# A decoder layer on one core: 96 instead of 64 tokens of the second group gather their experts, and 72 instead of 56 expert chunks run ahead of the second product

## The chip, the cores and the metric

The kernel runs on one core of one Trainium2 chip. TensorE (PE) multiplies matrices, VectorE (DVE), ScalarE (ACT) and GpSimd (POOL) do elementwise work, SyncE (SP) mostly issues DMAs, and sixteen DMA engines move data between HBM and the core's memories. The metric is device microseconds of one execution, from three runs. Each kernel's profile comes from one further execution.

## The reference, cut to what matters

One layer over 512 tokens of 2048 channels in f32: a mixer (pooling and attention heads in parallel), a cross attention over 256 memory tokens, and an expert layer (PEER), each added to x, and a last RMSNorm. The change lies mostly in PEER. For each token and each of 8 heads, two score vectors over 128 keys give the 16 best keys each, the 16 best sums of pairs give 16 experts of 16,384 (expert = key 1 x 128 + key 2) and a softmax over the 16 gives gates. With 128 experts k per token:

```python
a = jnp.einsum('td,tkd->tk', hb, jnp.take(w_u, ib, axis=0))
c = gb * jax.nn.gelu(a)
y = jnp.einsum('tk,tkd->td', c, jnp.take(w_v, ib, axis=0))
```

w_u and w_v are 16,384 x 2048 each, 134 MB. The attention rotates 32 of 128 channels of q and k by sines and cosines of the positions (rope).

## The kernel before, in words

**Two groups of tokens.** The first 128 tokens go through all layers first (row layout, from L370). The other 384 (`TR`) follow in a transposed layout `xT` (channels in partitions, 16 tiles `KD`).

**Two ways to do PEER.** *Gathering*: for a block of 128 rows, one indirect DMA fetches one expert row of 8 KB for each (1 MB in all, `rows`, L113), and DVE makes a dot product with the token (`dot0`, L318; `dot1`, L1075) or adds the scaled row to a sum in PSUM (`axpy0`, L331; `axpy1`, L1086). The first group does this for its 128 tokens: 128 dots, a turn with the GELU, 128 sums, an output step. Of the second group the first `NS` = 64 tokens do it too: each token stands in two rows (`SG` = 2), so 64 dots and 64 sums suffice. *Dense*: the other `ND` = 320 tokens are multiplied with all 16,384 experts, in 128 chunks of 128 experts, and a table of gates, zero for experts not chosen, masks the result.

**Products in three parts.** Each f32 weight tile of 128 x 1024 (`wraw`, 512 KB, four buffers, loaded by SP) is split into a high half (`wh`, ACT, L143) and a low half (`wl`, DVE or POOL, L144). `mm3` (L149 to L152) multiplies high by high, high by low, low by high. A w_u chunk (`proj_one`) has 48 such matmuls with `ND` moving columns, a group of w_v (8 chunks, 16 output tiles) has 384.

**Order of the stages of the second group.** Attention and pooling (`z_chunk`; the first group's pick, `pick0`, runs beside its start in steps of DVE), w_out, cross attention, the PEER query projection with its scores, and then:
- *Picks* (L1038 to L1061): for each of three blocks of 128 tokens, `pick` makes experts and gates on DVE, three transposes on PE bring them to row layout, and then `a_until` issues the next `KB` = 7 w_u chunks, whose GELU goes to DRAM (`gad`). Their low halves are made on POOL.
- *Gates* (L1105 to L1134): 80 steps of four tokens; DVE compares (L1114) and scales (L1116), PE multiplies (L1119), ACT stores (L1120), and the blocks go to DRAM (`gd`). The w_u chunks from 21 to `K1` = 56 run beside them.
- *Second product* (L1177 on): 16 groups of w_v, the groups of chunks 56 to 127 first. Beside a group the eight chunks of the next are prepared (`c_chunk`): for chunks from `K1` on, the w_u chunk itself; below, the activation is read back from `gad`. The gates come from `gd`. In the last group but one the gathered sums are transposed and added to `xT` (L1203 to L1210).

**The queue of gather steps.** `queue` (L342) is a list of closures, 258 for the first group and 131 for the second, and `behind(rate)` takes so many from it at places between the matmuls. `RATE` sets it by stage: 3.0 and 2.2 a chunk in attention and pooling (from the tenth chunk on), 2.5 in w_out, 2.0 in cross attention, 0.25 in the query projection and the picks, 1.2 in the gates and at the first eight chunks of the second product. After that, the rest is spread over the slots of the groups (16 a group), by 1.3 (`R2`) more than the mean in the groups that still carry w_u chunks (L1167 to L1170). Rows land in four buffers in turn: `x0`, `rowx` and a pool of two. From L1064 on POOL runs in program order; the other engines are ordered by the framework's planner.

**Sines.** `cosT` and `sinT` for rope are made at the start of the second group's attention (L757 to L767), right before the first use.

## Time and profile before

| | |
|---|---|
| median of 3 runs (lowest, highest) | 3175.05 us (3169.79, 3180.04) |
| profiled execution | 3175.37 us, span 3173.6 us |
| mean granted clock of PE | 0.968 |
| busy: PE, DVE, POOL, ACT | 93%, 76%, 45%, 41% |
| moved by DMA | 912.79 MB, mean 288 GB/s |
| queue 1, weights and stores (SP) | 471.21 MB |
| queue 0, gathers (POOL) | 402.68 MB |
| queue 10 (ACT) | 35.88 MB |

The profile shows one execution. "Busy" of PE counts pipelined matmuls, so two kernels' shares can't be compared with the peak; how far apart matmuls start is read from counts in a stretch. The granted clock is the share of 2.4 GHz that PE was given: 1 or, at 1.2 GHz, 0.5, and a mean between them over a stretch. The DMA share is the time that packets took, over the time of sixteen engines; packets that overlap can bring it a little over 1. In a row of windows, each engine has its busy time and, after an x, its count of instructions; PEclk, the DMA share and GB/s end the row. The line numbers are those of the kernel before.

### The profile page before, as it was taken

The numbers are of one execution on the slowest core, as the hardware profiler recorded it, in microseconds if no ns is written. First come the engines' busy times: TensorE is split into PE (matmuls) and PEld (weight loads), VectorE is DVE, ScalarE is ACT, GpSimd is POOL, SyncE is SP. The second block draws the span as 40 slices with busy tenths as digits, with TensorE's granted clock in tenths as the row PEclk, the third lists the DMA queues.
The fourth block names the chain that finished last, engine by engine and source line by source line (L and its number), as shares of the span: only waits on it lengthen the run. The fifth ranks groups of instructions, "written<-read, shape, count | busy, mean of one in ns | idle before, by whom it ended". The sixth has DMA issues, their size and how long they took to land.

```text
span 3173.6 us, 47405 instructions
## 1 busy us (share of the span) xinstructions
PE 2947.7 (93%) x18311; PEld 2832.5 (89%) x18311; DVE 2422.7 (76%) x3360; ACT 1298.6 (41%) x1789; POOL 1433.8 (45%) x826
## 2 busy tenths in 40 slices
PE   7999879998988997899998999999999999999997
PEld 5868769988978997899998999999999999899997
DVE  7797877798878579599894767777777678787756
ACT  5676534432344443355543333333433333233334
POOL 0000046644534665544546555555555554454532
PEclk9999989999989998999999999999999999999998
DMA  7886737888975344588888989999899999999953
GB/s 261 295 300 214 244 119 282 330 309 339 342 266 192 111 127 124 182 302 318 315 304 315 357 325 359 357 367 355 330 372 353 353 354 358 346 357 362 343 163 106
DMA packets 243521, 912.79 MB, mean 288 GB/s; under 512 B 23488, under 2 KB 85600, under 8 KB 192224
## 3 DMA queue, kind: packets, MB, share of 16 engines
q1 hardware_dynamic: 136304, 471.21, 42.2%
q0 software_dynamic: 55296, 402.68, 32.1%
q10 hardware_dynamic: 51696, 35.88, 3.7%
q8 instruction: 144, 2.36, 0.3%
q14 instruction: 81, 0.66, 0.1%
HBM read 874.22 MB, written 35.45 MB: 287 GB/s over the span
## 4 chain that ended last, share of the span: by engine, by line
PE 66%; DVE 20%; DMA 5%; issue 5%; ACT 2%; POOL 0%; ACTq 0%; POOLq 0%; DVEq 0%; SPq 0%
PE pm L150 11%; PE pm L152 11%; PE pm L151 11%; PE pa L152 9%; PE pa L150 9%; PE pa L151 9%; DVE wl L144 2%; DVE u L1114 2%; DVE oh L295 1%; DVE oh L293 1%; PE pm L400 1%; PE pm L401 1%; PE pm L399 1%; PE pa L1119 1%; DMA rows<-in_w_v_rows_dram,sidx 1%
## 5 line engine op out<-in xcount | busy, mean ns | idle before, releaser
L144 POOL TENSOR_TENSOR wl<-wraw,wh 128x1024 fp32r<-128x1024 f32 x369 | 930.5, 2526 | 1433.3 <-ACT wh L143 1401.4
L143 ACT ACTIVATE wh<-wraw 128x1024 fp32r<-128x1024 f32 (+1 forms) x658 | 693.7, 1058 | 1042.1 <-PE pm L151 467.0
L152 PE MATMUL pa<-ch,wl 128*128 128x320 f32 x2048 | 634.5, 312 | 25.4 <-DVE wl L144 23.5
L150 PE MATMUL pm<-dH,wh 128*128 128x320 f32 x2048 | 640.4, 313 | 15.0 <-DVE cl L1164 6.5
L152 PE MATMUL pm<-dH,wl 128*128 128x320 f32 x2048 | 640.6, 313 | 6.1 <-DVE wl L144 3.9
L150 PE MATMUL pa<-ch,wh 128*128 128x320 f32 x2048 | 636.7, 311 | 7.3 <-DVE xT L1193 4.7
L151 PE MATMUL pm<-dL,wh 128*128 128x320 f32 x2048 | 639.0, 312 | 0.0
L151 PE MATMUL pa<-cl,wh 128*128 128x320 f32 x2048 | 635.3, 310 | 0.0
L144 DVE TENSOR_TENSOR wl<-wraw,wh 128x1024 fp32r<-128x1024 f32 (+1 forms) x289 | 377.4, 1308 | 166.5 <-ACT wh L143 158.7
L152 PEld LDWEIGHTS pa<-ch,wl 128*128 128x128 f32 x2048 | 387.1, 189 | 30.4 <-DVE wl L144 28.1
L150 PEld LDWEIGHTS pm<-dH,wh 128*128 128x128 f32 x2048 | 389.2, 190 | 16.3 <-DVE cl L1164 6.8
L150 PEld LDWEIGHTS pa<-ch,wh 128*128 128x128 f32 x2048 | 388.3, 190 | 10.2 <-ACT ch L1163 5.2
L152 PEld LDWEIGHTS pm<-dH,wl 128*128 128x128 f32 x2048 | 389.3, 190 | 8.2 <-DVE wl L144 5.4
L151 PEld LDWEIGHTS pm<-dL,wh 128*128 128x128 f32 x2048 | 389.3, 190 | 0.0
L151 PEld LDWEIGHTS pa<-cl,wh 128*128 128x128 f32 x2048 | 388.1, 190 | 0.0
L150 PE MATMUL pm<-hH,wh 128*128 128x384 f32 x1024 | 355.9, 348 | 10.4 <-DVE k L811 3.4
L152 PE MATMUL pm<-hH,wl 128*128 128x384 f32 x1024 | 354.2, 347 | 10.5 <-DVE wl L144 10.5
L151 PE MATMUL pm<-hL,wh 128*128 128x384 f32 x1024 | 354.4, 346 | 5.2 <-DVE hL L874 4.4
L1193 DVE TENSOR_TENSOR xT<-pa,xT 128x320 f32<-128x320 f32 x256 | 124.7, 487 | 196.6 <-PE pa L152 191.0
L150 PEld LDWEIGHTS pm<-hH,wh 128*128 128x128 f32 x1024 | 197.6, 193 | 17.1 <-issue 5.8
L152 PEld LDWEIGHTS pm<-hH,wl 128*128 128x128 f32 x1024 | 197.6, 193 | 13.4 <-DVE wl L144 12.5
L151 PEld LDWEIGHTS pm<-hL,wh 128*128 128x128 f32 x1024 | 197.7, 193 | 6.9 <-DVE hL L874 4.7
(413 smaller groups left out, 4571.6 us busy)
## 6 DMA issues: line engine op xcount, KB each, us to landing
wraw<-in_w_u_dram SPq DMA_DIRECT2D x256, 512.0 KB
wraw<-in_w_v_dram SPq DMA_DIRECT2D x256, 512.0 KB
wraw<-in_w_in_dram SPq DMA_DIRECT2D x64, 512.0 KB
xT<-in_w_in_f_dram SPq DMA_DIRECT2D x63, 512.0 KB
gd<-stage SPq DMA_DIRECT2D x10, 2048.0 KB
gt<-gd ACTq DMA_DIRECT2D x32, 640.0 KB
wraw<-in_w_pq_f_dram SPq DMA_DIRECT2D x32, 512.0 KB
wraw<-in_w_out_dram SPq DMA_DIRECT2D x32, 512.0 KB
```

Of the source, the lines that this page charges most:

```text
L143: S.activation(wh[:, c], raw[:, c], AF.Copy)
L144: i = (lo_eng or V).tensor_tensor(wl[:, c], raw[:, c], wh.bitcast(F32)[:, c], op=ALU.subtract)
L150: TE.matmul(ps, wh, xh, start=start, stop=False)
L151: TE.matmul(ps, wh, xl, start=False, stop=False)
L152: TE.matmul(ps, wl, xh, start=False, stop=stop)
L293: V.tensor_tensor(oh, iota50.unsqueeze(1).broadcast_to([P, 16, NCAND]), cf[:, h, :].unsqueeze(2).broadcast_to([P, 16, NCAND]), op=ALU.is_e ...
L295: V.tensor_tensor(oh, oh, ecand[:, h, :].unsqueeze(1).broadcast_to([P, 16, NCAND]), op=ALU.mult)
L399: TE.matmul(ps, xh, wh, start=start, stop=False)
L400: TE.matmul(ps, xh, wl, start=False, stop=False)
L401: TE.matmul(ps, xl, wh, start=False, stop=stop)
L1114: V.tensor_tensor(u, iota.unsqueeze(1).unsqueeze(1).broadcast_to([P, 2, 4, P]), e12T[:, :, t:t + 4].unsqueeze(3).broadcast_to([P, 2, 4, P] ...
L1193: V.tensor_tensor(xT[:, dd, NS:], ps[:, :ND], xT[:, dd, NS:], op=ALU.add)
```

## The change

- `NS` goes from 64 to 96, `ND` from 320 to 288, and the gate blocks `NTB` from 10 to 9. The 96 tokens gather in two sets: 64 tokens in two rows each (64 dots, 64 sums) and 32 in four rows each (32 and 32). Each set starts by reading its repeated tokens from DRAM (`hyd`) and ends in a row buffer; the first set's sums are added after two dots of the second (`add1`).
- `K1` goes from 56 to 72 and `KB` from 7 to 9. In the picks, `a_until` now stands ahead of the transposes, which are ordered after the last matmul issued. A new rate, 0.5, holds for the chunks in the picks.
- The repeated tokens are made by POOL and ACT, not by DVE, and go to DRAM.
- `cosT` and `sinT` are made in the first group's PEER query projection.
- In `pick0` the product with the one-hot comparison runs on POOL.

```diff
-NS = 64
-SG = P // NS
-NK = P // SG
+SETS = ((0, 64), (64, 32))
+NS = sum(n for _, n in SETS)
-RATE = (3.0, 2.2, 2.5, 2.0, 0.25, 1.2)
+RATE = (3.0, 2.2, 2.5, 2.0, 0.25, 0.5, 1.2)
-K1, U0, GE = 56, 0, 2
-KB = 7
+K1, U0, GE = 72, 0, 2
+KB = 9
@@ mm3
-        TE.matmul(ps, wl, xh, start=False, stop=stop)
+        last_mm[0] = TE.matmul(ps, wl, xh, start=False, stop=stop)
@@ pick_steps (eng is G from pick0, V else)
-            V.tensor_tensor(oh, oh, ecand[:, h, :].unsqueeze(1).broadcast_to([P, 16, NCAND]), op=ALU.mult)
+            eng.tensor_tensor(oh, oh, ecand[:, h, :].unsqueeze(1).broadcast_to([P, 16, NCAND]), op=ALU.mult)
@@ the first group's PEER query projection (the lines at the attention's start go)
+        def pos_in():
+            posr.append(ep.tile([P, TR], F32, name="jk", bufs=2)[:32].bitcast(I32))
+            nc.scalar.dma_start(posr[0], a["positions"][:, T0:].broadcast_to([32, TR]))
+            nc.scalar.dma_start(invf, a["invfreq"])
+        def trig_rows():
+            V.tensor_copy(cosT, posr[0])
+            V.tensor_scalar(cosT, cosT, scalar1=invf, scalar2=None, op0=ALU.mult)
+            trig(cosT, ep.tile([P, TR], F32, name="jk", bufs=2)[:32], sinT, cosT)
+            V.tensor_scalar(sinT[0:16], sinT[0:16], scalar1=-1.0, scalar2=None, op0=ALU.mult)
+        hooks_x[2][0] = [pos_in]
+        hooks_x[2][5] = [trig_rows]
@@ a_chunk
-        ps = proj_one(a["w_u"][j], dH, dL, ND, lo_eng=lo, rate=RATE[4] if j < RB * KB else RATE[5] if j < K1 else 0)
+        ps = proj_one(a["w_u"][j], dH, dL, ND, lo_eng=lo, rate=RATE[5] if j < RB * KB else RATE[6] if j < K1 else 0)
@@ picks
+            a_until(KB * b + KB)
             pt = pa.tile([P, 512], F32, name="pa")
-            TE.transpose(pt[:, 0:P], e12[:, 0, :], ident)
...
+            with tc.issue_after(last_mm[0].ins):
+                TE.transpose(pt[:, 0:P], e12[:, 0, :], ident)
...
-            a_until(KB * b + KB)
@@ the second group's gather steps
+    def start1(s):
         gx[0] = gxp.tile([P, D], F32, name="gx")
-        S.copy(gx[0], hy1)
+        r = row_tile()
+        nc.sync.dma_start(r, hyd[s])
+        S.copy(gx[0], r)
+    def end1(s):
+        ys[s] = row_tile()
+        S.copy(ys[s], gx[0])
+    def add1(s):
+        o, n = SETS[s]
         for k4 in range(4):
             pt = pa.tile([P, 512], F32, name="pa")
             for kk in range(4):
+                TE.transpose(pt[:, kk * P:(kk + 1) * P], ys[s][:, (4 * k4 + kk) * P:(4 * k4 + kk + 1) * P], ident)
+            x = xT[:, 4 * k4:4 * k4 + 4, o:o + n]
+            for g in range(P // n):
+                V.tensor_tensor(x, pt.rearrange("p (k g t) -> p k g t", k=4, t=n)[:, :, g, :], x, op=ALU.add)
+    for s, (o, n) in enumerate(SETS):
+        ks, at_ = range(o, o + n), len(queue) + 3
+        queue += [lambda s=s: start1(s)] + [lambda k=k: dot1(k) for k in ks] + [lambda c=slice(o, o + n): turn1(c)]
+        queue += [lambda k=k: axpy1(k) for k in ks] + [lambda s=s: end1(s)]
+        if s:
+            queue.insert(at_, lambda s=s - 1: add1(s))
@@ repeated tokens
-                for g in range(SG):
-                    V.scalar_tensor_tensor(out=hn[:, g, :], in0=xT[:, k, :NS], scalar=gains[:, 3, k:k + 1], in1=r2c[:, :NS], op0=ALU.mult, op1=ALU.mult)
+                G.tensor_tensor(hx, xT[:, k, :NS], r2c[:, :NS], op=ALU.mult)
+                    S.activation(hn, hx[:, o:o + n].unsqueeze(1).broadcast_to([P, P // n, n]), AF.Copy, scale=gains[:, 3, k:k + 1])
...
+                hs4 = gw.tile([P, 512], F32, name="hs4", bufs=3)
+                S.copy(hs4, pt)
+                nc.scalar.dma_start(hyd[s, :, k4 * 512:(k4 + 1) * 512], hs4)
@@ last group but one
-                    for kk in range(4):
-                        TE.transpose(pt[:, kk * P:(kk + 1) * P], y1[0][:, (4 * k4 + kk) * P:(4 * k4 + kk + 1) * P], ident)
...
+                add1(len(SETS) - 1)
```

## Rows read from the trace of the kernel before

**Rows 1.** Page: the span in 40 slices, busy tenths of PE and DMA.

```profile
PE   7999879998988997899998999999999999999997
...
DMA  7886737888975344588888989999899999999953
```

**Rows 2.** Page: the chain that ended last, shares of the span by engine.

```profile
PE 66%; DVE 20%; DMA 5%; issue 5%; ACT 2%; POOL 0%; ACTq 0%; POOLq 0%; DVEq 0%; SPq 0%
```

**Rows 3.** Windows: stretch, length; busy PE, PEld, DVE, ACT, POOL; clock; DMA.

```profile
380.00:460.00 80.00, 57.66 (x279) 53.22 (x280) 70.20 (x212) 27.10 (x48) 32.30 (x21) 0.79 0.37 121
1145.00:1300.00 155.00, 123.52 (x774) 121.03 (x773) 150.69 (x367) 49.96 (x63) 89.36 (x33) 0.88 0.40 123
1300.00:1690.00 390.00, 371.45 (x2626) 366.83 (x2625) 327.43 (x282) 187.02 (x209) 195.37 (x91) 0.98 0.82 301
1690.00:2658.00 968.00, 952.27 (x6440) 950.18 (x6439) 685.16 (x650) 342.63 (x420) 525.11 (x314) 0.99 0.92 350
2658.00:3035.00 377.00, 350.97 (x2311) 344.41 (x2310) 297.78 (x306) 121.78 (x148) 184.49 (x107) 0.98 0.93 345
3035.00:3152.00 117.00, 114.25 (x776) 112.86 (x774) 62.53 (x95) 55.40 (x99) 36.03 (x15) 1.00 0.41 126
```

**Rows 4.** Windows in which PE never stops: 320 columns, then 384 columns.

```profile
2030.00:2090.00 60.00, 60.00 (x411) 60.00 (x410) 42.70 (x38) 21.02 (x25) 32.79 (x20) 1.00 0.92 346
790.00:845.00 55.00, 55.00 (x313) 55.00 (x312) 40.74 (x44) 16.29 (x19) 26.64 (x18) 1.00 0.92 353
```

**Rows 5.** DMA, 1745 to 2658: packets, MB, share of 16 engines.

```profile
q0 software_dynamic: 23989, 174.77, 47.5%
q1 hardware_dynamic: 36580, 133.20, 39.6%
q10 hardware_dynamic: 20851, 12.59, 4.7%
```

**Rows 6.** DMA, 2658 to 3035.

```profile
q0 software_dynamic: 8555, 62.22, 41.2%
q1 hardware_dynamic: 13956, 50.85, 36.5%
q10 hardware_dynamic: 23904, 16.55, 14.5%
```

**Rows 7.** Windows: a whole group, the best 10 us, and a turn between sets.

```profile
2314.00:2427.00 113.00, 112.72 (x768) 112.26 (x766) 83.56 (x94) 39.73 (x49) 60.91 (x38) 1.00 0.96 375
2210.00:2220.00 10.00, 10.00 (x71) 10.00 (x70) 7.58 (x8) 3.93 (x5) 2.35 (x3) 1.00 1.02 419
2280.00:2290.00 10.00, 10.00 (x70) 10.00 (x70) 5.92 (x13) 7.07 (x9) 5.76 (x3) 1.00 0.69 249
```

**Rows 8.** Groups by line: count, busy us, mean ns of one, idle before it.

```profile
L144 POOL TENSOR_TENSOR wl<-wraw,wh 128x1024 fp32r<-128x1024 f32 x369 | 930.5, 2526 | 1433.3 <-ACT wh L143 1401.4 <-PE pa L152 12.2 <-DVE gx L331 9.3
L144 DVE TENSOR_TENSOR wl<-wraw,wh 128x1024 fp32r<-128x1024 f32 x287 | 376.0, 1312 | 165.1 <-ACT wh L143 157.3 <-issue 7.3
L331 DVE SCALAR_TENSOR_TENSOR gx<-rows,sact,gx 128x2048 f32<-128x2048 f32 x64 | 150.3, 2349 | 21.4 <-DMA rows<-in_w_v_rows_dram,sidx 16.2 <-issue 4.8
L1114 DVE TENSOR_TENSOR u<-iota,e12T 128x1024 f32<-128x1024 f32 x80 | 119.9, 1517 | 0.7 <-PE pa L1119 0.7
L1119 PE MATMUL pa<-u 128*128 128x128 f32 x640 | 86.3, 281 | 17.2 <-DVE u L1116 14.7 <-ACT stage L1120 2.1 <-ACT ga L1026 0.4
L1116 DVE TENSOR_TENSOR u<-u,gT 128x512 f32<-128x512 f32 x80 | 72.4, 917 | 0.3
L295 DVE TENSOR_TENSOR oh<-oh,ecand 128x800 f32<-128x800 f32 x24 | 45.3, 1922 | 0.0
L1101 DVE SCALAR_TENSOR_TENSOR hn<-xT,gains,r2c 128x64 f32<-128x64 f32 x32 | 9.3, 345 | 4.3 <-PE pa L1102 4.2
```

**Rows 9.** Timeline of PE near 410: start, us, engine, line; idle before, releaser.

```profile
411.68 1.22 PE L818 MATMUL pa<-kT,q 128*128 128x128 f32 x4 [13.33 <-POOL q L776]
```

**Rows 10.** Waits of PE, 1145 to 1310: us in total, times, longest.

```profile
PE pa L1054 <- DVE e L1052: 20.8, 3, 11.0
```

73 lines of the change are left out of this document (31 added, 42 removed).

## The prediction

> **What bounds the kernel now.** I read the 40 slices first: TensorE (PE) stands at 9 nearly throughout, with dips in slices 6 and 16, while the DMA row is near 9 all through the last half and falls to 3 before it [rows 1]. The chain of waits agrees: two thirds of it is PE, a fifth VectorE (DVE), little DMA [rows 2]. So PE bounds on average, but the change works in stages with different limits, and those are read from a table of windows [rows 3].
> - 380 to 460: PE 58 of 80 us at a granted clock of 0.79. One wait of 13.3 us stands in it, the first scores waiting for a rotated q [rows 9].
> - 1145 to 1300, the three picks beside the first dense chunks: DVE is busy for 151 of 155 us, PE 124 at clock 0.88. PE waits 20.8 us, three times, for the picks' indices [rows 10], because a transpose that needs them stands in PE's order before the next seven chunks.
> - 1300 to 1690, the gate tables: PE 371 and DVE 327 of 390.
> - 1690 to 2658, the eight groups whose w_v work carries w_u chunks: PE 952 of 968, DMA share 0.92.
> - 2658 to 3035, the groups with w_v alone: PE 351 of 377, DMA 0.93. Here PE already stops.
> - 3035 to 3152, two groups without gathers: DMA 0.41.
> All sums are made against the profiled execution, 3175.37 us: a span of 3173.6 and 1.8 around it. The median of the runs, 3175.05, is the same to 0.3 us, so I add nothing.
>
> **Narrower products.** At full clock 411 matmuls start in 60 us with 320 columns and 313 in 55 us with 384 [rows 4]: 146.0 and 175.7 ns, in both 0.457 ns a column. 288 columns make 132 ns; a floor from weight loading would show as more than proportional time, and with two widths on one line I see none. A chunk (48 matmuls) falls from 7.0 to 6.34 us, a group of w_v (384) from 56 to 50.7. Over 12,288 matmuls that is 172 us of PE time, if PE is what everything waits for.
>
> **More gathers.** Thirty-two more tokens cost 64 more gathers of 1 MB, each one DMA and one DVE step of 2.35 us [rows 8]. By the rates in the code, the steps taken before the first of the last w_u chunks are 98.6 up to the query projection, 4 in it, and then 21 x 0.25 + 35 x 1.2 = 47.25 before, 27 x 0.5 + 45 x 1.2 = 67.5 after: 150 of 389 before, 170 of 457 after. Left are 240 before and 287 after (8 of them no gathers). The pacing gives 1.322 and then 0.655 a slot before (16 slots a group), 1.581 and 0.966 after.
>
> What they cost the DMA engines: in 1745 to 2658 (913 us) the gather queue moved 174.8 MB in 47.5% of the engines' time [rows 5], 2.60 us of all sixteen for 1.049 MB; weights took 39.6% for 133.2 MB, 1.42 us for a half chunk of 0.524 MB; the rest is 4.7%, 5.4 us a group. In 2658 to 3035 the same prices are 2.62 and 1.42, and gate tables with stored activations take 14.5%, 9.1 us in each of six groups [rows 6]. These last shrink by a tenth.
> - First kind of group, six instead of eight: 25.3 gathers x 2.60 + 32 x 1.42 + 4.8 = 116 us of DMA, against 101.4 of PE. DVE's 685 us [rows 3] are 80 a group now, 50 of them gather steps; with 25.3 x 2.35 it is 90.
> - Second kind, eight with gathers: 15.45 x 2.62 + 16 x 1.42 + 8.2 = 71.4 of DMA, against 50.7 of PE. DVE's 298 us are 50 in each of the six groups, half of them gather steps; with 36 it is 61.
> So in both DMA takes PE's place as the bound; before, the same sums are 105 against 113 and 59 against 56. Let s be the DMA share that the stage keeps up. Then it lasts (6 x 116 + 8 x 71.4 - 20)/s + 158, where 20 are the eight steps that gather nothing, and 158 the first eight w_u chunks (52) and two last groups (117 x 132/146 = 106). That is 1247/s + 158. For s the trace has 0.96 as the best whole group and 1.02 in the best 10 us [rows 7]. I take 0.985, between them, as transfers that are always late are always queued: 1424 us, where 1690 to 3152 took 1462: **-38**. Ends: 1471 at 0.95 (+9), and 1380 at 1.02 (-82). The full PE saving of this stage, 9600 x 0.146 - 8832 x 0.132 = 236 us, is mostly not had.
>
> **The picks and the sixteen chunks moved ahead.** Waits on the picks go, since nine chunks (57 us of PE) now precede each pick's transposes. Late next is DVE: its 151 us stay, 8 more gather steps add 19, and GpSimd, which makes both low halves of each chunk (2 x 2.53 us of 6.34), is now busy four fifths of the time, not 89 of 155. The one-hot products measure 1922 ns [rows 8], where their 800 elements at the gather step's pace would be 920; I read the excess of 1 us as a wait for GpSimd. Over 24 such products and the 24 comparisons of the same shape it may double (+48) or stay; I take +12, a quarter, as GpSimd's share rises by about that. That ends the picks after 182 us, where 27 chunks of PE need 171; before, the 21 chunks took until 1329, 184 us.
> Gate tables: nine blocks, not ten, so 72 steps x 2.43 us, with 54 gather steps and 45 low halves x 1.31: 361 us of DVE. PE: 45 x 6.34 + 576 x 0.135 = 363. Before, 80 x 2.43 + 42 x 2.35 + 35 x 1.31 and the 9 of the repeated tokens, which leave DVE, made 348 of DVE in the 361 us to 1690, 4% less than they took. So 376 now, and 182 + 376 = 558 for what took 545: **+13**. Ends: -15 if PE's floor holds alone (171 + 363 = 534, a little less waiting), +60 if contention doubles and both engines wait in turns. Moved work costs its stores too: sixteen more writes of 147 KB on SyncE's queue behind the chunk's activation, hidden while four weight buffers stand ahead.
>
> **Early sines, and the product on GpSimd.** The positions' load and the chain of sines leave the place where rope waits for them, so the 13.3 us wait [rows 9] shrinks to what q itself needs. Late next is DVE, which is full there. In their new place, the query projection of the first group (slices 4 and 5, where PE is at 9 and 8), ten DVE instructions cost between 3.5 us (345 ns each, the shortest of rows 8) and 9 (917 ns); half hidden, I price them at 3. Eight one-hot products leave DVE for GpSimd, where rope is queued: from -10 to +8; I take -2. Together **-12**, between -20 and +5.
>
> **The second set's turns.** Each set reads its tokens through DRAM into a row buffer, copies them to PSUM, and begins anew. At such a turn now the gather queue is empty for some 10 us: share 0.69 for 0.93 [rows 7]. Here are two more turns (end and start, dots to sums); behind each, gathers, DVE's steps, and so GpSimd's next issues wait, and the load of the tokens can hold SyncE's weight loads behind it while it waits for a row buffer. From 2.4 us (the lost share) to 13 us each; two make **+12**. The adds of the first set (16 transposes, eight small adds) lie in DMA's time; repeating the tokens on ScalarE and GpSimd lies beside DVE's gates, which have the longer time.
>
> Sum: -38 + 13 - 12 + 12 = -25, **3150 us**.
>
> **Rivals.**
> 1. The forecast: DMA-bound groups, 3150, own range 3120 to 3180. For it: PE already idles in 2658 to 3035 at share 0.93. Against: that is under the 0.96 of a group in which PE didn't stop, so transfers alone can't be what stops it.
> 2. Slower: two queues and in-order DVE steps let the share reach no more than 0.95, as in the w_v groups now, where gathers and weights take turns in being late. Other terms make +13, so the change pays only while 1247/s + 158 is under 1449, s over 0.966. At 0.95 it is 3197, at 0.93 3225. For it: no whole group passed 0.96. Against: none of them had more demand than the engines give.
> The Trainium skill (DMA: Bandwidth & Descriptors, Where 436 GB/s comes from) has HBM transfers of one core bound at about 358 GB/s. By an estimate from that page and the groups' 44.5 and 27 MB they would take 124 and 75 us, 3212 in all. The trace disagrees: 375 GB/s over a group with PE undisturbed [rows 7].
> 3. Better: late transfers pack closer than their mean durations, s = 1.04, a little past the 10 us peaks: 3083. For it: the peaks reach 419 GB/s. Were DMA no bound at all, DVE and PE would end at 6 x 101.4 + 8 x 61 + 158 = 1254, 2980.
> 4. TensorE slows itself. In the w_v groups PE would have work for 50.7 of 72 us. Where it stood still as much (58 of 80 us), the granted clock was 0.79 [rows 3], that is 1.2 GHz for four tenths of the time. At 0.79 a group needs 64 us of PE, still hidden; it decides below 0.70, and at 0.6 eight groups cost 84 each: +92, 3242. Against: in 2658 to 3035 the clock held 0.98.
> The Trainium skill (TensorE: Matmul & The Clock Gate, Part 1) says that the throttled level is the default and activity releases it; with DMA as the bound that rule speaks against this change.
> 5. The picks stage doesn't do what is said: GpSimd's low halves bound it, PE waits as before, so that the excess doubles: 48 in the place of 12 on the picks, 3186, and 3176 where half of it is made up in the gates: no change or slightly slower.
>
> **How the numbers follow.** Chances: forecast 0.45, rival 2 0.22, rival 3 0.16 (0.03 of it near 2980), rival 4 0.07, rival 5 0.10. A measurement tells some 0.3% from no change, 3165.5 to 3184.6. Faster: three quarters of the forecast (0.34), all of rival 3, 0.03 of others: 0.53. No change: 0.08 of the forecast, 0.06 of rival 5, 0.03 of rival 2: 0.17. Slower: 0.30. The range leaves out half of rival 3 below 3085 and rival 4 with the tail of 2 above 3225; the forecast's own range is 3120 to 3180.
>
> **What would show it.** Matmuls of 288 columns 132 ns apart; groups of 115 to 120 us (first kind) and 71 to 77 (second) at DMA 0.97 or more; PE under 0.8 busy in the w_v groups; the first c chunk near 1690; no wait on the picks' indices over 15 us in total; the wait at the first scores gone. Wrong: w_v groups near 60 us, or a DMA share under 0.95 with PE idle.

## The result: 5.4% slower, and the profile after

The changed kernel takes 3352.0 us (median of four runs, 3343.9 to 3354.4), the kernel before 3176.2 beside it: ratio 1.0543, 95% interval 1.0520 to 1.0566. I had forecast 3150, between 3085 and 3225. Its profiled execution took 3353.05 us, with a span of 3351.2 and a mean granted clock of 0.929 (before 0.968).

The page's slices after, for [rows 1] (PE's clock is shown too):

```profile
PE   7989799989889997898999988889888778878787
...
PEclk8999999999999998999999999999899888888898
DMA  7886649879865454787899998989889989898963
```

The last third has PE at 7 and 8 with a lower clock, and DMA still near 9. The chain by engine, for [rows 2]:

```profile
PE 56%; DVE 25%; issue 8%; DMA 4%; ACT 3%; POOL 2%; ACTq 0%; DVEq 0%; SPq 0%; POOLq 0%
```

PE's part falls from 66% to 56%, DVE's rises from 20% to 25%. The stages, for [rows 3] (length; busy us and count of PE, weight loads, DVE, ACT, POOL; granted clock, DMA share, GB/s):

```profile
1136.00:1344.00 208.00, 175.00 (x1223) 171.55 (x1223) 154.84 (x341) 70.00 (x90) 129.54 (x49) 0.91 0.48 148
1344.00:1371.00 27.00, 21.69 (x108) 15.71 (x108) 0.36 (x1) 18.13 (x42) 12.64 (x18) 0.75 0.46 151
1371.00:1763.00 392.00, 359.37 (x2661) 351.12 (x2660) 336.06 (x246) 175.60 (x204) 203.35 (x95) 0.98 0.87 328
1929.00:2578.00 649.00, 559.46 (x3860) 552.12 (x3860) 482.29 (x440) 200.35 (x249) 329.77 (x205) 0.92 0.90 345
2578.00:3212.00 634.00, 495.31 (x3069) 478.97 (x3068) 501.90 (x485) 160.02 (x197) 279.68 (x184) 0.85 0.91 337
3212.00:3330.00 118.00, 109.31 (x782) 107.43 (x782) 74.44 (x109) 57.54 (x102) 39.66 (x17) 0.96 0.45 145
```

The last three rows are five of the six groups with w_u chunks (129.7 us each; 114.7 before), eight with w_v alone and gathers (79.3; [rows 3] has 62.8), and two without gathers. By the end of a GELU on ScalarE or of a group's last addition, the two profiled executions differ so:

| stretch | before | after | measured | forecast |
|---|---|---|---|---|
| start to the first dense chunk | 1153.1 | 1135.7 | -17 | -12 |
| picks (21 and 27 chunks) | 176.8 | 207.7 | +31 | |
| to the first chunk beside the gates | 7.6 | 27.2 | +20 | |
| to the first chunk of the second product | 347.2 | 398.0 | +51 | the three: +13 |
| second product | 1467.1 | 1561.2 | +94 | -38 and +12 |

So the forecast missed by 88 us in the middle and by 120 in the second product. There the transfers' demand is what I had worked out. The queues of the two stretches (packets, MB, share of sixteen engines), for [rows 5, 6]:

```profile
q0 software_dynamic: 17865, 130.11, 50.4%
q1 hardware_dynamic: 23235, 85.10, 35.2%
q10 hardware_dynamic: 12069, 8.12, 4.0%
...
q0 software_dynamic: 17213, 125.29, 50.7%
q1 hardware_dynamic: 18576, 68.17, 29.6%
q10 hardware_dynamic: 29216, 19.62, 10.1%
```

A gather costs 0.504 x 649 us x 1.0486 / 130.11 = 2.64 us of all engines (2.60 forecast), a half chunk 1.41. With a share of 0.90, a group's demand is 0.90 x 649 / 5 = 117 us; in the eight others 0.91 x 634 / 8 = 72 (forecast 116 and 71.4). What failed is the share: 0.90 and 0.91, where I took 0.985 and gave the low case 0.95. And PE did stop, mostly for low halves (waits: engine, tile, line, releaser; us in total, times, longest; first the five groups, then the eight):

```profile
PE pa L156 <- DVE wl L146: 83.3, 20, 7.6
...
PE pa L156 <- DVE wl L146: 83.0, 37, 4.0
```

PE was not busy for 89.5 and 138.7 us, and 83 of each are these waits; in [rows 3]'s groups it was busy for all but 16 of 968 and 26 of 377 us. How one stop comes about, in the timeline (start, us, engine, line; idle before, releaser):

```profile
2411.62 0.40 ACT L1034 ACTIVATE pm<-pm 128x288 f32<-128x288 f32 x1 [5.47 <-PE pm L156]
...
2412.05 0.47 DVE L1192 TENSOR_TENSOR pm<-pm,gt 128x288 f32<-128x288 f32 x1 [0.83 <-ACT pm L1034]
...
2412.42 2.28 DVE L1087 CUSTOM_DVE_ANT_0 rows<-rows,gx 128x2048 f32<-128x2048 f32 x1
...
2412.84 2.97 ACT L145 ACTIVATE wh<-wraw 128x1024 fp32r<-128x1024 f32 x3
...
2414.62 0.45 DVE L1197 TENSOR_TENSOR cl<-pm,ch 128x288 fp32r<-128x288 f32 x1
...
2414.98 5.70 POOL L146 TENSOR_TENSOR wl<-wraw,wh 128x1024 fp32r<-128x1024 f32 x2 [3.79 <-ACT wh L145]
2414.99 0.45 DVE L1226 TENSOR_TENSOR xT<-pa,xT 128x288 f32<-128x288 f32 x1
...
2415.14 0.29 PE L155 MATMUL pm<-dL,wh 128*128 128x288 f32 x1
2415.36 3.06 DVE L146 TENSOR_TENSOR wl<-wraw,wh 128x1024 fp32r<-128x1024 f32 x1
...
2418.45 0.33 SPq L144 DMA_DIRECT2D wraw<-in_w_v_dram  x1
...
2418.48 0.40 PE L156 MATMUL pa<-ch,wl 128*128 128x288 f32 x1 [3.04 <-DVE wl L146]
```

ScalarE stands 5.5 us at a GELU, waiting for PE's last matmul of the chunk, with the next three high halves behind it in its order. When these come, at 2412.8 to 2415.8, VectorE is in a gather step; then come a difference and an addition, and only then the low half that PE needs. By then GpSimd has begun its own low halves, and VectorE's takes 3.06 us, not 1.2. PE has no more work at 2415.4 and goes on at 2418.5. And SyncE issues the next load of a weight only then, as the late low half frees its buffer: a late bunch can make the next one late. (ScalarE's waits at GELUs alone are no news: 148.7 us in these 649, and 144.3 in 908 before, where the low halves still came in time.)

Gathers wait for buffers too. GpSimd issues one when VectorE has freed a row buffer, and its low halves stand behind that issue in its order (the largest such wait of the eight groups):

```profile
POOL rows L116 <- DVE gx L1098: 92.4, 30, 5.6
```

Over all row buffers GpSimd's waits for VectorE add up to 148 us in the five groups and 235 in the eight; in 1745 to 2658 and 2658 to 3035 before, to 27 and 2. The engines seldom wait for a transfer itself: VectorE for gathered rows 3 and 8 us in the two stretches, ScalarE for weights 22 and 27. No run gives the gathers more row buffers, so what this wait is worth by itself stays open.

The long low half is no single case. In 1935 to 2578 VectorE made 80: 62 of them overlapped one on GpSimd by less than 5% and took 1.22 us on average, the 7 overlapped by more than 80% took 3.11; the other 11 lie between, at 1.4 to 4.5. Over the whole page the mean rose from 1312 ns [rows 8]:

```profile
L146 DVE TENSOR_TENSOR wl<-wraw,wh 128x1024 fp32r<-128x1024 f32 (+1 forms) x283 | 431.6, 1528 | 139.6 <-ACT wh L145 138.8
```

The Trainium skill (SBUF — State Buffer, SBUF: two separate sides) has a VectorE instruction with two operands from SBUF and a GpSimd instruction that reads SBUF take a shared pair of ports for the whole instruction, the later one waiting. The trace agrees: GpSimd's first low half began at 2414.98 and, at some 2.4 us each, ended near 2417.4; VectorE's own 1.2 us after that give the 2418.4 seen.

### The profile page after: what moved, and what is told of

Read it like the earlier page. It is cut to its first block, busy times and chain, and to the rows that moved or that the text cites. A ratio compares the mean times of both kernels' runs of the same rounds, so it can differ in the third digit from the quotient of the medians.

```text
span 3351.2 us, 47738 instructions
## 1 busy us (share of the span) xinstructions
PE 2906.7 (87%) x18279; PEld 2762.8 (82%) x18279; DVE 2589.5 (77%) x3412; ACT 1292.4 (39%) x1821; POOL 1542.4 (46%) x920
## 4 chain that ended last, share of the span: by engine, by line
PE 56%; DVE 25%; issue 8%; DMA 4%; ACT 3%; POOL 2%; ACTq 0%; DVEq 0%; SPq 0%; POOLq 0%
PE pm L156 9%; PE pm L154 9%; PE pm L155 9%; PE pa L156 8%; PE pa L154 7%; PE pa L155 7%; DVE wl L146 6%; DVE u L1147 2%; DVE gx L335 2%; POOL wl L146 1%; DVE u L1149 1%; DVE gx L1098 1%; PE pm L405 1%; PE pm L404 1%; PE pm L406 1%
## 5 line engine op out<-in xcount | busy, mean ns | idle before, releaser
L156 PE MATMUL pa<-ch,wl 128*128 128x288 f32 x2048 | 663.6, 325 | 186.2 <-DVE wl L146 173.1
L154 PE MATMUL pa<-ch,wh 128*128 128x288 f32 x2048 | 654.3, 320 | 45.5 <-ACT wh L145 24.5
L155 PE MATMUL pa<-cl,wh 128*128 128x288 f32 x2048 | 650.6, 318 | 0.0
L156 PE MATMUL pm<-dH,wl 128*128 128x288 f32 x2048 | 620.6, 303 | 28.5 <-POOL wl L146 15.7
L154 PE MATMUL pm<-dH,wh 128*128 128x288 f32 x2048 | 617.1, 302 | 30.1 <-ACT wh L145 23.9
L155 PE MATMUL pm<-dL,wh 128*128 128x288 f32 x2048 | 615.8, 301 | 0.0
L146 DVE TENSOR_TENSOR wl<-wraw,wh 128x1024 fp32r<-128x1024 f32 (+1 forms) x283 | 431.6, 1528 | 139.6 <-ACT wh L145 138.8
L154 PEld LDWEIGHTS pa<-ch,wh 128*128 128x128 f32 x2048 | 432.8, 211 | 51.8 <-ACT wh L145 29.6
L1226 DVE TENSOR_TENSOR xT<-pa,xT 128x288 f32<-128x288 f32 x256 | 116.2, 454 | 205.9 <-PE pa L156 204.4
L116 POOL DMA_INDIRECT rows<-in_w_v_rows_dram,sidx x112 | 129.9, 1160 | 173.1 <-DVE gx L1098 89.5
```

Of the source, the lines that this page charges most:

```text
L116: G.indirect_dma_start(out=dst, out_offset=None, in_=src, in_offset=bass.IndirectOffsetOnAxis(ap=idx, axis=0))
L146: i = (lo_eng or V).tensor_tensor(wl[:, c], raw[:, c], wh.bitcast(F32)[:, c], op=ALU.subtract)
L154: TE.matmul(ps, wh, xh, start=start, stop=False)
L155: TE.matmul(ps, wh, xl, start=False, stop=False)
L156: last_mm[0] = TE.matmul(ps, wl, xh, start=False, stop=stop)
L1226: V.tensor_tensor(xT[:, dd, NS:], ps[:, :ND], xT[:, dd, NS:], op=ALU.add)
```

## The experiments

Where nothing else is said, a kernel was run once, beside the kernel before, and a difference under some 15 us between two such runs is not read. Groups of the first kind carry w_u chunks, those of the second have w_v alone. In the texts quoted, "first chunk of the second product ... 1735" was misread: its GELU ends at 1768.6 in the changed kernel, and at 1684.7 before.

| kernel | us | first kind | second kind |
|---|---|---|---|
| changed | 3352 | 129.7 | 79.3 |
| half_step | 3309 | 126.9 | 74.6 |
| half_rows | 3086 | 106.9 | 61.4 |
| five_bufs | 3358 | 128.7 | 80.3 |
| copy_act | 3352 | 129.9 | 77.7 |
| eight_raw | 3416 | 127.5 | 85.8 |
| dve_lows | 3318 | 131.2 | 67.6 |
| one_set | 3185 | 113.6 | 67.4 |
| early_undo | 3349 | 130.6 | 78.3 |
| early_lows | 3343 | 126.6 | 77.7 |
| strict_lows | 3325 | 124.6 | 75.1 |
| strict_half | 3100 | 107.1 | 62.0 |
| highs_first | 3289 | 122.5 | 75.0 |
| keep_clock | 3447 | 135.2 | 80.7 |
| r2_17 | 3329 | 144.8 | 62.6 |
| after_all | 3243 | 119.6 | 71.7 |

### Steps or transfers: half_step, half_rows

```diff
@@ half_step: dots and sums in the second product, all three closures alike
+        c = slice(0, D if paced[0] else D // 2)
-        V.scalar_tensor_tensor(out=gx[0], in0=r, ..., in1=gx[0], ...)
+        V.scalar_tensor_tensor(out=gx[0][:, c], in0=r[:, c], ..., in1=gx[0][:, c], ...)
@@ half_rows
+        if not paced[0]:
+            rows(r[:, D // 2:], a["w_v_rows"].rearrange("e (h d) -> (e h) d", h=2), sidx2[:, k:k + 1])
+            r2 = r[:, D // 2:].unsqueeze(2).broadcast_to([P, D // 2, 2])
...
```

> The changed kernel, but in the second product every gather step of VectorE works on 1024 of the 2048 columns; the gathers still fetch whole rows (this leaves half of the dots and sums out). Theory A (VectorE's fixed order: gather steps stand ahead of the next low half, TensorE stops, its clock falls): the steps fall from 2.35 to about 1.2 us, the stops at low halves go, groups of the first kind come down from 130 us to about 112 to 118 and of the second from 79 to 70 to 73, where the transfers end it; total 3170 to 3230. Theory B (the transfers bound the groups): the groups stay at 125 to 132 and 75 to 82, total 3330 to 3360.

> The changed kernel, but in the second product each gather fetches 1024 of the 2048 columns and VectorE's step reads each fetched element twice, so that it stays 2048 elements long (dots and sums are then of half rows). Theory A (VectorE's order): the demand on the DMA engines falls by 25.3 x 1.3 = 33 us in a group of the first kind and 20 in one of the second, and the time hardly moves: groups of 122 to 132 and 74 to 82 us, total 3310 to 3360. Theory B (transfers): groups of 102 to 108 and 55 to 62, total 3050 to 3130.

Measured: 3309 and 3086, the first between its two theories, the second in theory B. The windows of half_step, first and second kind:

```profile
1935.00:2570.00 635.00, 552.11 (x3840) 545.10 (x3840) 354.42 (x442) 197.77 (x249) 333.79 (x205) 0.94 0.92 351
2570.00:3166.00 596.00, 478.62 (x3087) 461.01 (x3088) 369.19 (x486) 159.76 (x198) 277.90 (x184) 0.90 0.95 360
```

DVE has 128 us less to do in the first kind and 133 in the second, and PE stops as before. Those of half_rows:

```profile
1928.00:2462.00 534.00, 521.11 (x3853) 516.39 (x3853) 456.98 (x439) 202.18 (x250) 338.46 (x206) 1.00 0.85 298
2462.00:2954.00 492.00, 437.05 (x3094) 423.25 (x3094) 481.46 (x487) 161.29 (x196) 294.60 (x183) 0.98 0.88 307
```

In the first kind PE is nearly always busy, and the clock is back at 1.00 and 0.98. Theory A, my first, falls: the length of VectorE's steps is worth 43 us, the bytes 266. But the planner had also ordered the engines anew, by its own estimate of the times. A stretch of VectorE's order (LOW a low half, g a gather step, mul the gate product, cl the difference, add the addition to xT):

```
changed:     mul g cl add LOW g add g LOW LOW mul add cl g LOW add g g mul g cl add LOW g add g mul cl g add LOW LOW LOW add
half_rows:   LOW g LOW g mul add LOW g add cl g g LOW mul g add cl add g LOW g LOW mul add LOW g cl add
strict_lows: LOW g g LOW mul add cl g add g g add LOW mul LOW cl g add LOW g g add g LOW mul cl g add g LOW mul cl
```

With fewer bytes the low halves stand singly and early; with all of them, in bunches behind products and steps.

### The order held: early_lows, strict_lows, strict_half

```diff
@@ early_lows: the loads of the second product in a list, made two half chunks ahead of their use
+        while todo and len(ready) < 3:
+            ready.append(load_now(*todo.pop(0)))
+        return ready.pop(0)
@@ strict_lows: also
-    paced[0] = False
+            with tc.issue_after(anchor[0].ins):
+                V.tensor_tensor(ga..., gts[j // 4][:, :, j % 4, :], op=ALU.mult)
@@ strict_half: strict_lows with half_rows' gathers
```

> The changed kernel, but each weight load of the second product with its two halves is issued two half chunks earlier in the program (before the product of the half chunk two places ahead), so that VectorE's low halves stand earlier in its order; no buffer and no byte is added. In the changed kernel VectorE's order has low halves in bunches behind a gate product, up to two gather steps and an addition; where gathers were halved the low halves stood singly, ahead of those. Theory O (this order makes the stops): part of the low halves move ahead, groups of 120 to 127 and 73 to 79 us, total 3230 to 3310. Theory T (whole transfers end the groups, whatever the order): total 3335 to 3365.

> As the last one, and VectorE's gate products and gather steps of the second product are also ordered behind the newest low half that VectorE makes, so that none of these low halves waits for them. Theory O: stops at low halves under a fifth of the 107 us that 1735 to 2590 shows in the changed kernel; then the transfers bound the groups as forecast, 115 to 121 and 71 to 75 us, total 3180 to 3240. Theory T: groups stay at 126 to 132 and 75 to 82, total 3330 to 3370. A third way: gather steps wait behind low halves whose weights are late, row buffers come free later, the DMA share falls: over 3370.

> The last one with gathers of half rows in the second product (steps of whole length; half of each row is left out). With the order nearly held, this shows what the bytes alone are worth. Theory T: as with half rows before, 3070 to 3110, and well over 150 us below the last run. Theory O: the last run is already near what the transfers allow, and this one lies 60 to 130 us below it: groups of 103 to 108 and 56 to 64 us, total 3070 to 3130. Were the order all, the two would be the same.

Measured: 3343, 3325 and 3100. The first total lies in theory T, though its groups are those of theory O; the second is just under T's range and far above O's. Under an order that is much the same, half the bytes are worth 225 us (theory T), this order itself 27. So transfers decide first.

### More room: five_bufs, eight_raw

```diff
@@ five_bufs: high and low halves alternate between two pools of three and two
+        pool = wq[wn[0] % len(wq)]
@@ eight_raw: raw weights alternate between two pools of four
+        raw = wq[wn[0] % len(wq)].tile([P, 1024], F32, name="wraw", bufs=WRAW)
```

> The changed kernel, but with five buffers each for the high and the low halves of the weights in the second product, in the place of three. Theory A (VectorE's order): low halves can be made two half chunks (6.3 us of TensorE) earlier, so that one or two gather steps ahead of them cost nothing: stops of TensorE at low halves fall to a third, groups to about 115 to 122 and 71 to 75 us, total 3200 to 3290. Theory B (transfers bound the groups, the order does not matter): total 3330 to 3360. If the four raw buffers limit how early a half can be made, little changes in A either.

> The changed kernel, but with eight buffers for the raw weights in the second product in the place of four, so that each load can be issued some 13 us of TensorE's time earlier. Halving the gathers' bytes gave 3086 us, halving VectorE's steps only 3309: transfers decide. Theory L (each weight load comes late, since four buffers allow too little time while 1 MB gathers are ahead of it): the DMA share rises from 0.90 to 0.97 or more, groups fall to 114 to 120 us (first kind) and 70 to 74 (second), total 3180 to 3260. Theory T (the memory gives no more than some 345 GB/s to this mix): groups stay at 126 to 132 and 75 to 84, total 3330 to 3360.

Measured: 3358 and 3416. More halves gave nothing, though one whole group ran as forecast, at a share of 0.99 and full clock:

```profile
1931.00:2043.00 112.00, 103.58 (x760) 101.26 (x758) 91.29 (x73) 39.00 (x48) 65.97 (x43) 1.00 0.99 393
```

With eight raw buffers the first kind gains 2 us a group and the second loses 6; both theories missed it. In the first kind ScalarE waits for no weight any more, so late loads (theory L) are not what held it. In the second kind ScalarE's waits for PE to free a high half's buffer grow from 145.6 us to 333.4 (last line below), but why the kernel is slower stays open. More raw buffers and more halves were not tried together.

```profile
1951.00:2589.00 638.00, 558.68 (x3840) 545.79 (x3838) 473.77 (x441) 203.82 (x250) 326.69 (x203) 0.93 0.92 348
2589.00:3275.00 686.00, 514.21 (x3069) 492.09 (x3070) 538.89 (x481) 159.88 (x194) 281.68 (x185) 0.85 0.85 311
...
ACT wh L147 <- PE pa L157: 333.4, 89, 9.4
```

### GpSimd without low halves: dve_lows

```diff
-        lo = G if j < RB * KB else (V, G) if j < K1 else G if j < K1 + GRP or j % 2 == 0 else V
+        lo = G if j < RB * KB else (V, G) if j < K1 else V
-                wh, wl = load_w(a["w_v"][g, dd], lo_eng=G if dd % 2 else V)
+                wh, wl = load_w(a["w_v"][g, dd], lo_eng=V)
```

> The changed kernel, but in the second product VectorE makes all low halves and GpSimd none. In the changed kernel a low half on VectorE takes 1.22 us, but 3.1 where one on GpSimd runs at the same time, and the stops of TensorE end with such long ones. Theory P (these meetings make the stops): no low half over 1.4 us, groups of 118 to 126 and 70 to 76 us, total 3220 to 3310. Rival (VectorE's load: 16 more low halves, 20 us more in each group of the first kind, 10 in the second): groups of 132 to 140 and 82 to 90, total 3380 to 3450. Third (transfers alone, VectorE has room): 3330 to 3370.

Measured: 3318. The first row is three groups of the first kind, the second three of the second kind in which no gather ran:

```profile
2263.00:2644.00 381.00, 332.84 (x2304) 315.98 (x2304) 364.28 (x340) 116.46 (x145) 139.41 (x97) 0.98 1.02 406
2727.00:2886.00 159.00, 156.59 (x1155) 155.52 (x1156) 103.63 (x152) 62.29 (x76) 0.00 (x0) 0.99 0.69 218
```

With nothing between its issues, GpSimd let gathers run ahead of the plan, 32 a group (33.5 MB), at a share of 1.02 and 406 GB/s for 381 us. So 0.90 is no ceiling of the chip. The first set ended early, and then no gather ran for three groups, until the second set began: there PE was the bound and the share 0.69. Theory P missed, the total (3220 to 3310) by 8 us and the groups on both sides. No low half is long here, yet in the three groups of the first row PE still waits 48 us for low halves, so their meetings on the two engines are not the whole cause; their own part isn't shown, since the gathers moved too.

The Trainium skill's 358 GB/s (DMA: Bandwidth & Descriptors, Where 436 GB/s comes from), by which my estimate was 124 and 75 us a group, lies near the 129.7 and 79.3 measured at 345 and 337 GB/s. The 406 GB/s here rule it out as the cause; they agree with another page of the Trainium skill (Perfetto Trace Analysis, Roofline), by which one core working alone may exceed 358 and is bounded by its sixteen engines at about 435.

### The 64 gathers: one_set

```diff
-SETS = ((0, 64), (64, 32))
+SETS = ((0, 64),)
```

> The changed kernel with the first set of tokens alone: 64 tokens gather and the dense products have 320 columns as before; all else (72 chunks ahead, early sines, order of the picks, repeated tokens through DRAM) stays. By the sum's terms a group of the first kind then has 100 us of transfers for 112 of TensorE, one of the second 63 for 56. Theory (64 more gathers cost the second product its time): groups of 112 to 115 and 62 to 67 us, the first chunk of the second product at 1760 to 1795 (wider chunks, ten gate blocks), total 3150 to 3210. Rival (another part, as the order of the engines or the new turns, costs the time): groups of 120 or more and 72 or more, total over 3260.

Measured: 3185, within the theory, 11 us above the kernel before beside it; the second kind, at 67.4, just misses it.

```profile
1939.00:2507.00 568.00, 564.42 (x3847) 563.89 (x3846) 390.38 (x380) 205.52 (x248) 297.94 (x176) 1.00 0.91 341
2507.00:3046.00 539.00, 482.97 (x3083) 469.25 (x3082) 420.14 (x448) 159.00 (x196) 257.22 (x156) 0.96 0.93 345
```

Without the second set PE hardly stops in the first kind and less in the second (56 of 539 us); the clock is back at 1.00 and 0.96. So the second set, 64 gathers of 1 MB, turned a product bound by PE into one bound by transfers; narrower products (112 to 101 us a group) could not pay for it.

### The stops themselves: highs_first, keep_clock

```diff
@@ highs_first: for all weight tiles of the second product
+        for k in range(8):
+            TE.matmul(ps, wh[:, c[k]], xh[k], start=start and k == 0, stop=False)
+            TE.matmul(ps, wh[:, c[k]], xl[k], start=False, stop=False)
+        for k in range(8):
+            TE.matmul(ps, wl[:, c[k]], xh[k], start=False, stop=stop and k == 7)
@@ keep_clock: ahead of each w_v tile's product
+                for _ in range(8):
+                    TE.matmul(ps[:, :ND], cs[0][0][:, :P], cs[0][0], start=True, stop=True)
```

> The changed kernel, but in the second product each weight tile's sixteen matmuls with the high half come first and the eight with the low half after, where before they alternated (a low half was needed from the third matmul on). TensorE can then go on 14 x 0.132 = 1.85 us longer before it needs a low half, and no byte, step or buffer changes. Theory C (the stops of 3 to 7 us push TensorE to half clock, and in these stretches the transfers fall to 0.69 of their engines, so that shorter stops give back more than they save): half clock under 5% of the groups in the place of 16 and 29%, groups of 116 to 122 and 71 to 75 us, total 3220 to 3280. Theory T (the transfers' own pace is what falls short, the clock only follows): under 15 us gained, total 3335 to 3360.

> The changed kernel with eight more matmuls of 288 columns at the head of each of the 16 tiles of a group (their result is overwritten), 16 x 8 x 0.132 = 17 us more work for TensorE in a group, which has 101 and 51 us of its own and took 130 and 79. Theory C (half clock costs some 10 us a group): the clock stays over 0.97 and groups are no longer than 118 to 128 and 72 to 78 us, total 3260 to 3350, faster with more work. Theory T or the order of the engines: the 17 us add wholly or in half, total 3400 to 3550.

Measured: 3289 and 3447. The windows of highs_first:

```profile
1936.00:2549.00 613.00, 542.96 (x3840) 537.27 (x3838) 479.42 (x441) 196.80 (x247) 328.65 (x205) 0.95 0.93 363
2549.00:3149.00 600.00, 474.92 (x3102) 458.34 (x3103) 502.24 (x485) 161.95 (x198) 286.43 (x184) 0.90 0.95 357
```

Not a byte less, 1.85 us more patience at each low half, and 63 us are gone; the share rises to 0.93 and 0.95. This is far from theory T and 9 us above theory C (3220 to 3280), whose sign came only in part: 1.2 GHz holds for 10% and 20% of the two stretches, not under 5%, and PE still waits 58 and 55 us for VectorE's low halves. The windows of keep_clock:

```profile
1954.00:2630.00 676.00, 630.25 (x4473) 621.51 (x4474) 471.40 (x440) 198.91 (x249) 327.30 (x206) 0.95 0.87 330
2630.00:3276.00 646.00, 582.75 (x4122) 569.83 (x4120) 492.89 (x486) 161.28 (x197) 273.90 (x184) 0.96 0.91 333
```

The 17 us of added work lengthen a group by 5.5 and 1.4 us only, so most of it fits into stops, and the clock rises from 0.92 and 0.85 to 0.95 and 0.96. But nothing is given back, in the second kind either, where the clock comes back most: the clock alone isn't the cause. By the trace's clock records the changed kernel had 1.2 GHz for 16% of 1930 to 2578, and there the transfers ran at 0.69, against 0.94 in the rest; from 2578 to 3212 it was 29%, with 0.91 in both. So in the first kind loads and gathers fall back while PE is slow after a stop, and in the second they don't; that the slow clock causes the first is not shown, as keep_clock speaks against it.

### Bunched gathers: r2_17

```diff
-R2 = 1.3
+R2 = 1.7
```

> The changed kernel with the gather steps spread otherwise: 1.7 times the mean in the groups that carry w_u chunks in the place of 1.3, and so 2.07 a slot there and 0.63 after, for 1.58 and 0.97; the sum stays. By transfers a group of the first kind then needs 33.1 x 2.60 + 50.2 = 136 us and one of the second 10.1 x 2.62 + 30.9 = 57, against 51 of TensorE. Theory (a share of some 0.92 where transfers bound, and near TensorE's time where they don't): 5 x 148 + 8 x 60 = 1220 us in these groups, where the changed kernel took 1283: total 3270 to 3310. Rival (VectorE's 33 steps a group, 78 us on top of 40, make it the bound): groups of 155 or more, total over 3350.

```profile
1970.00:2694.00 724.00, 588.33 (x3823) 568.25 (x3822) 556.55 (x479) 196.71 (x247) 361.86 (x243) 0.88 0.95 363
2694.00:3195.00 501.00, 444.34 (x3090) 433.66 (x3090) 382.68 (x443) 162.16 (x199) 240.04 (x140) 0.94 0.90 335
```

3329: 23 us better, 20 short of the theory. Where 33 gathers fall into a group the share is 0.95; eight groups then need 62.6 us.

### The early stages: copy_act, early_undo, before_early

In the changed kernel two waits stand in the middle: ScalarE's at the copy of a pick's gates, and VectorE's for the first gather beside the gates.

```profile
1261.69 0.39 ACT L1034 ACTIVATE ga<-pm 128x288 f32<-128x288 f32 x1
1287.25 0.27 ACT L1071 COPY gT<-pa 128x128 f32<-128x128 f32 x1 [25.18 <-DVE e12T L1070]
...
1289.05 1.99 ACT L145 ACTIVATE wh<-wraw 128x1024 fp32r<-128x1024 f32 x2
...
1371.11 2.29 DVE L322 CUSTOM_DVE_ANT_0 rowx<-rowx,gx 128x2048 f32<-128x2048 f32 x1 [26.75 <-DMA rowx<-in_w_u_rows_dram,sidx]
```

```diff
@@ copy_act
-            V.tensor_copy(e12T[:, :, ts_], pt...)
+            S.copy(e12T[:, :, ts_], pt...)
@@ early_undo: transposes ahead of a_until again, and for the repeated tokens
-                G.tensor_tensor(hx, xT[:, k, :NS], r2c[:, :NS], op=ALU.mult)
-                    S.activation(hn, hx[:, o:o + n]..., AF.Copy, scale=gains[:, 3, k:k + 1])
+                    V.scalar_tensor_tensor(out=hn, in0=xk, scalar=gains[:, 3, k:k + 1], in1=rk, op0=ALU.mult, op1=ALU.mult)
@@ before_early: the kernel before with the diff's sines and pick0's eng=G
```

> The changed kernel, but the transposed expert indices of a pick are copied out of PSUM by ScalarE and not by VectorE. In the changed kernel ScalarE waits 25 us twice at the copy of the gates, behind VectorE's copy, which stands after the next pick's 24 products, and the weights of the next chunk wait behind it on ScalarE. Theory A2 (this order cost the picks stage some 45 us): the two pauses of 31 and 27 us between chunks fall under 12 each, the first chunk of the second product starts at 1690 to 1705 in the place of 1735, total 3300 to 3320. Theory B2 (VectorE's whole work in the picks is the bound, the pauses only show it): the pauses come back at another place, the first chunk starts at 1720 to 1735, total 3335 to 3360.

> The changed kernel with two parts of the early stages undone: in the picks the transposes stand ahead of the nine chunks again, and the repeated tokens are made on VectorE, as 32 instructions, not on GpSimd and ScalarE. Theory E (the chunks put ahead leave VectorE without gate work after the last pick, and GpSimd's share of the repeated tokens stands ahead of the next gathers, for whose first row VectorE waits 27 us): VectorE's idle time between 1290 and 1371 (about 75 us) falls by half or more, the first chunk of the second product starts at 1685 to 1705 in the place of 1735, total 3300 to 3325. Rival (VectorE's sum of work decides when the gates end): the first chunk starts at 1725 to 1740, total 3335 to 3360.

> The kernel before with two parts of the change alone: sines made in the first group's query projection, and pick0's one-hot product on GpSimd. In the changed kernel the first dense chunk's activation ends at 1135.7 us against 1153.1 before; theory: these 17 us stay, 3152 to 3164 (ratio 0.993 to 0.997). Rival: VectorE's gates and gathers take them back later, 3168 to 3180 (ratio 0.998 to 1.002).

copy_act: 3352, nothing gained. The pause came back at the next instruction of ScalarE that needs the pick, the exponential of its gates:

```profile
1258.34 0.37 ACT L1070 COPY e12T<-pa 128x256 f32<-128x256 f32 x1 [0.24 <-PE pa L1067]
...
1283.13 0.31 ACT L305 ACTIVATE gt<-gt 128x128 f32<-128x128 f32 x1 [22.95 <-DVE gt L304]
```

VectorE ends its three picks at 1284 to 1290 in the kernel before, in the changed one and in this, and ScalarE's order lets no weight past the last pick's exponential. PE has done the eighteen chunks of the first two picks by 1262 and stands; the last nine then run with little for VectorE to do. Theory B2 holds.

early_undo: 3349; the 27 us before the first gate chunk became 7, but the gate stage took 408 us, so that the second product began 8 us earlier, where 30 to 50 were forecast. The rival holds.

before_early (three rounds): 3169.6 us for 3176.5, ratio 0.9971 (0.9951 to 0.9991). The first dense chunk comes 16 us earlier, and the time falls by some 9 (3 to 16 by the interval), by the ratio between the two theories: about half is taken back.

### What is left: after_all, best1, best2

after_all joins strict_lows, highs_first and early_undo. best1 is before_early with highs_first, best2 adds strict_lows to it.

> The changed kernel with all that helped or might: low halves made early and ahead of gate products and gather steps, matmuls with the high halves first, the picks' transposes ahead of the nine chunks and the repeated tokens on VectorE. Theory C (stops, order and half clock hold the share under the forecast's 0.985): a share of 0.97 or more in the groups, 117 to 121 and 71 to 75 us, total 3200 to 3250, still slower than before, because the transfers then bind as in the forecast and the early stages take the rest. Theory T (the mixture of gathers and weights gets no more than 0.94): groups 122 to 126 and 74 to 78, total 3260 to 3300.

> The kernel before (64 tokens gather, 56 chunks ahead) with the early sines, pick0's product on GpSimd, and in the second product all matmuls with a high half ahead of those with the low half. The kernel before has stops at low halves only in the groups with w_v alone (61 to 65 us for 56 of TensorE). Theory: these groups fall to 57 to 60 us, six of them give 20 to 30 us, with 9 us of the early stages: 3130 to 3155. Rival (transfers end these groups, their 59 us of demand at 0.95): 3160 to 3172.

> The best so far (64 tokens, early sines, high halves first; 3155 us, ratio 0.9938) with the low halves also made two half chunks earlier and gate products and gather steps behind them. Its groups with w_v alone take 60 to 64 us at a share of 0.97, the others 112 to 114, TensorE's own time. Theory (nothing is left there but transfers): 3145 to 3160, the same. Rival (stops at low halves still cost 4 to 7 us in each of six groups): 3125 to 3145.

after_all: 3242.5, within theory C.

```profile
1925.00:2523.00 598.00, 541.59 (x3842) 532.76 (x3842) 470.05 (x438) 196.79 (x247) 336.70 (x203) 0.96 0.96 374
2523.00:3097.00 574.00, 464.78 (x3094) 443.42 (x3094) 499.99 (x483) 160.54 (x196) 298.83 (x185) 0.94 0.97 370
```

The groups take 119.6 and 71.7 us at shares of 0.96 and 0.97; the forecast had 116 / 0.985 = 117.8 and 71.4 / 0.985 = 72.5. So the forecast's bound is real and within reach of the hardware, and what kept the changed kernel from it is the order in which the engines feed PE. Even so it is slower than before, and 92 us above the forecast: its second product takes 1455 us, where 1467 - 38 + 12 = 1441 were forecast, and the other 77 are lost ahead of it.

best1 (three rounds): 3155.4 us for 3175.6, ratio 0.9938 (0.9919 to 0.9957), 0.6% faster than the kernel before. The total is at the theory's upper end (3155), but the second kind keeps 62 us as in the rival, where the theory had 57 to 60.

```profile
1838.00:2637.00 799.00, 792.12 (x5378) 791.34 (x5378) 587.58 (x556) 283.69 (x344) 444.52 (x259) 1.00 0.93 353
2637.00:3011.00 374.00, 345.81 (x2303) 339.25 (x2302) 308.23 (x304) 120.17 (x146) 185.87 (x107) 1.00 0.93 344
```

best2: 3186.5 for 3181.3, ratio 1.0019 (1.0001 to 1.0038), slower than best1; theory (3145 to 3160) and rival (3125 to 3145) both missed it. The loss is in the second kind, 67.5 us for 62.4 (the first kind has 114.9 for 114.1). There ScalarE waits longer, in its order, for VectorE's gate products, which now stand behind low halves (best1: 92.5 us in 27 waits); that this is the cause was not tested.

```profile
ACT ch L1195 <- DVE pm L1191: 205.3, 46, 7.4
```

## Why the prediction was wrong, point by point

- **The share (failed).** "For s the trace has 0.96 as the best whole group and 1.02 in the best 10 us [rows 7]. I take 0.985, between them, as transfers that are always late are always queued": it was 0.90 and 0.91, with PE idle, which the prediction itself named as a sign of being wrong. The reason given doesn't hold, as loads and gathers are queued only when a buffer comes free. PE stops, and my sum let it stop for nothing but the bytes. Instead ScalarE, VectorE and GpSimd, each in a fixed order, hand weights on late and in bunches (GELU, gather step, addition, then two low halves at once), and meanwhile weight and row buffers stay full and transfers idle. That the order and PE's patience hold the share down is shown by highs_first and after_all, which leave every byte and come to 0.93 to 0.97; that the bytes bring PE to stop at all, by half_rows, strict_half and one_set. Not shown is how much each link has in it (shared ports, row buffers, clock), nor by which wait the bytes lead to the stops, as the engines seldom wait for a transfer itself. Against the sum this is 60 us in the first kind and 54 in the second; the last two groups, at a share of 0.45, took another 11 that are not explained by it.
- **The prices of the demand (right).** 132 ns a matmul, 2.64 us a gather, 117 and 72 us a group.
- **Rival 2** had the right side and place, and the right point from which it decides (0.966), but ended at 0.93. 1247 / 0.905 + 158 would have been 1536 of the 1561 us.
- **Rival 4** had a clock of 0.79 in the w_v groups still hidden behind the transfers. It was 0.85 there, and 0.92 in the first kind; keep_clock, which brought it back and gained nothing, bears the rival's "still hidden" out.
- **Picks and gates: +13 forecast, +101 measured (failed).** The move of the chunks took away PE's wait for the indices [rows 10], but ScalarE's copy and exponential wait for the same picks: VectorE ends the third 150 us after the first chunk, PE the eighteen chunks of the first two after 126. The repeated tokens "beside DVE's gates" stood ahead of them: GpSimd, in program order, makes them before it issues the next gather, and VectorE, in order, waits 26.75 us for that row. And the chunks didn't lie under the gates: the tables were done at 1691, and the last ten of the 45 chunks came after them.
- **Rival 5** had the stage but not the mechanism: the one-hot products took 1812 ns, less than the 1922 of [rows 8], with GpSimd busier, so the excess was no wait for GpSimd. Its 3176 doesn't follow either: half of 36 us made up is 3168.
- **Sines (right in size):** -17 for -12; the 13.3 us wait of [rows 9] is gone. Half of it is worth nothing in the end (before_early).
- **The sets' turns: +12 forecast, none seen.** The group in which the second set begins (2818 to 2893) took 75.3 us beside 73.4 and 79.4.

## What to carry to other kernels

Trading matmuls for gathers doesn't pay where the bytes nearly fill the DMA engines. Before such a move, add up the transfers per group, and don't count on 0.98 of the engines: this kernel, whose weights pass through three in-order engines with a few microseconds of buffer, kept up 0.90, and 0.96 with its order mended. If it must be near that bound, let the consumer need the late half last (highs_first: a change of order in one loop, 63 us here). Whether keeping the two engines that make the halves off each other's ports pays is not shown: dve_lows did so and gained 34 us, but its gathers moved as well. A wait that is removed from one engine's order is worth looking for in the next engine's.

## What the runs showed of the hardware

- Sixteen DMA engines moved 406 GB/s for 381 us of gathers of 8 KB rows and 512 KB weight loads; I had taken 419 for a 10 us peak [rows 7].
- The same low half on VectorE took 1.22 us alone and 3.11 beside GpSimd's.
- Eight buffers for raw weights in the place of four made the kernel 64 us slower, which no theory here explains.
